# One more slot ahead of GpSimd's roots, and a residual load in sixteen pieces

## The chip, the cores and the metric

One core of a Trainium2 chip runs the kernel. The metric is device time in microseconds for one execution, from the start of the program to its end. A profile of one further execution shows what each engine did: PE (TensorE, matrix products; its weight loads are listed as PEld), DVE (VectorE), ACT (ScalarE), POOL (GpSimd), and SP (SyncE), which issues nearly all transfers.

## The reference

One layer of a hybrid streaming encoder is computed for 320 tokens: 256 of a new stream and 64 of a running one, model width 2048.

```python
h = rmsnorm(x, g_pre_mix)
p = h @ w_in                         # conv value and gate, q, k, v, z, two gates per head
a_out = conformer_conv(...)          # GLU, causal conv of width 31, LayerNorm per group, swish
b_out = gdn_mixer(...)               # gated delta rule, 8 heads of 128, chunks of 64
x = x + rmsnorm(concat(a_out, b_out) @ w_out, g_post_mix)
h = rmsnorm(x, g_pre_ffn)
gu = causal_dwconv(h @ w_up, ...)    # width 3
x = x + rmsnorm((silu(gate) * up) @ w_down, g_post_ffn)
```

Three pieces matter here. In the conv heads, eight groups of 128 channels are normalised per token: `(u - mu) * rsqrt(var + EPS)`. In the delta rule q and k are divided by their lengths, and its small matrices are scaled by `-beta` over the square of k's length. The output projection is followed by a norm, and then x, the residual stream, is added. All is fp32 in and out.

## The kernel before, in words

Each fp32 operand of a dense product is held as a rounded part (`whi`, `hh`, `bh`, ...) and a remainder (`wlo`, `hl`, `bl`, ...), and a product is three matmuls: hi by hi, hi by lo, lo by hi. Weights arrive by SP (L189) in blocks of 256 to 512 KB; ACT rounds a block to `whi` (L196), DVE subtracts to get `wlo` (L197). Three buffers hold raw blocks, three hold each split part, so the load of a block waits until `wlo` of the block three before it is done.

The order of the stages: the input projection, block by block (tiles psq, psv, psgate; up to about 433 us); the output projection `w_out` in two passes, the first with 11 of 16 k-blocks (psm, L212 to L216, up to about 512 us), the second with the last five (psm2, printed as psm, L999 to L1001); a norm; `w_up` with its conv; `w_down`; the last norm.

Everything that isn't a dense product runs as side jobs, written as generators. `tick` counts dense matmuls; after each 20 (GAP), it steps those jobs that are due. `yield wait, g, t` ends a step: the next one follows at the first count of 20 that is `wait` matmuls later, if g and t PSUM buffers of two pools can be held. What a step issues is then put in each engine's order by a scheduler that weighs its own estimates; what the engines run is one fixed list each, in order. So an instruction that waits holds all that stand behind it on its engine.

Four side jobs count here. `conv_tail` (one for each conv group, c0 to c7): three transposes into pt_c, statistics on DVE (L535, L536), EPS and the power -1/2 on GpSimd (L538, L539, tile grs), `gnm` on DVE (L541), three scalings on ACT (un, L544); after LAG_STAT = 100 matmuls, transposes back (pt_c2, L548), a swish on ACT (af, L550) and its split, bh on ACT (L220) and bl on DVE (L221), which the output projection reads. `gdn_tail` (eight heads, each in one or two parts; L645 runs eight times): transposes, square sums, EPS on DVE (L638, L639, tile tq), the power on GpSimd (L641, tile sc), small products on GpSimd (irk L643, cc L644, skd L646), snb on DVE (L645), scalings on ACT (kd L649, vh L654), matmuls pk and pks (L658, L662). The pair jobs solve the chunks (wi, np, tmp, dn: L666 to L706; zs L735, px L739, rhs L822, pvns L830, po L809 to L811, ks L839). `post` multiplies the heads' outputs by a root that GpSimd makes (L867 to L871), with the scalings at L873.

In the second pass of `w_out`, SP also carries x for the residual add (tile x1, L989), the first two blocks of `w_up` (printed with L189), and the parameters fpar of the next stage (L991). PSUM holds two psm2 blocks at a time: block n starts when DVE has added block n - 2 to its first half (m, L1007).

```python
hi, lo = load_split(ins["w_out2"][n], nk2 * P)
if n in (4, 8):
    upw.append(up_weights(len(upw), ugp))
```

Of the kernel before, what the change touches and what calls it, by code (L numbers as in the profile page):

```python
# [9 lines left out]
F32 = mybir.dt.float32  # L10
F32R = mybir.dt.float32r
AF = mybir.ActivationFunctionType
ALU = mybir.AluOpType
# [4 lines left out]
P = 128  # L18
D = 2048
KB = D // P  # L20
# [3 lines left out]
NH = 8  # L24
# [6 lines left out]
GAP = 20  # L31
# [8 lines left out]
LAG_NORM = 120  # L40
LAG_WAIT = 12
# [60 lines left out]
def trunk_kernel(ctx, tc, ins, outs):  # L102
    nc = tc.nc
# [188 lines left out]
    with tc.tile_pool(name="xp", bufs=1) as xp:  # L292
# [25 lines left out]
        with tc.high_priority(offset=PRI_E):  # L318
# [25 lines left out]
            for k in range(KB):  # L344
                x = xt[k // 4][:, k % 4, :]
# [52 lines left out]
    def gates():  # L398
# [54 lines left out]
        for t in (beta, eG, kdec):  # L453
            G.tensor_copy(t[0:TS, 2, 1:NH:2], t[0:TS, 2, 0:NH:2])
        G.tensor_scalar(neG, eG, -1.0, None, ALU.mult)
        for c, h0, w in ((0, 0, 4), (1, 0, 4), (2, 0, 8), (0, 4, 4), (1, 4, 4)):
            rg = gd.tile([P, 512], F32, tag="wtp", name="rg")
            eg = gd.tile([P, 512], F32, tag="wtp", name="eg")
            n = 512 // w
            if c < 2:  # L460
                rg3, mask = rg.rearrange("p (h i) -> p h i", i=n), cv("tri").unsqueeze(1).to_broadcast((P, w, n))
                g3 = gt[:, c, h0:h0 + w].unsqueeze(2).to_broadcast((P, w, n))
            else:
                rg3 = rg.rearrange("p (a b i) -> p a b i", b=2, i=n)
                mask = cv("tri2").rearrange("p (b i) -> p b i", b=2).unsqueeze(1).to_broadcast((P, 4, 2, n))
                g3 = gt[:, c, :].rearrange("p (a b) -> p a b", b=2).unsqueeze(3).to_broadcast((P, 4, 2, n))
            V.tensor_tensor(rg3, mask, g3, ALU.mult)
            yield LAG_DECAY, 1, 0
            psd = ps_g.tile([P, 512], F32, tag="g", name="psd")
            PE.matmul(psd, cv("strict"), rg, start=True, stop=True)  # L470
            S.activation(eg, psd, AF.Exp)
            for j in range(w // 2):
                if c < 2:
                    m = cv("tri").unsqueeze(1).to_broadcast((P, 2, n))
                else:
                    m = cv("tri2").rearrange("p (b i) -> p b i", b=2)
                V.tensor_tensor(E2[h0 // 2 + j][:, :, c * P:c * P + n],
                                eg[:, 2 * j * n:2 * (j + 1) * n].rearrange("p (b i) -> p b i", b=2), m, ALU.mult)
        gate.update(beta=beta, eG=eG, neG=neG, kdec=kdec, eGl=eGl, E=E)

    nqkv = const.tile([P, 24, 2, 3], F32, tag="nqkv", name="nqkv")

# [41 lines left out]
    def conv_tail(b, cvt, left):  # L524
# [13 lines left out]
        G.tensor_scalar(rs, gv[:, :, 1], EPS, None, ALU.add)  # L538
        G.tensor_tensor(rs, rs, nhalf[:, 0:3], ALU.pow)  # L539
        nm = cb.tile([P, 3], F32, tag="gnm", name="gnm")  # L540
        V.scalar_tensor_tensor(nm, gv[:, :, 0], -1.0, rs, ALU.mult, ALU.mult)  # L541
        un = cb.tile([P, 3, P], F32, tag="un", bufs=1, name="un")
        for c in range(3):
# [60 lines left out]
    def gdn_tail(h, st, kq, vT):  # L604
# [37 lines left out]
        rk, rq, irk, snb, cc, skd = (sc[:, i, :] for i in range(6))  # L642
        G.tensor_tensor(irk, tq6[:, 0, :], rk, ALU.mult)  # L643
        G.tensor_tensor(cc, rk, gate["beta"][:, 0:nch, h], ALU.mult)  # L644
        V.scalar_tensor_tensor(snb, cc, -1.0, rk, ALU.mult, ALU.mult)  # L645
        G.tensor_tensor(skd, rk, gate["kdec"][:, 0:nch, h], ALU.mult)  # L646
        for c in range(nch):
            if c < 2:
# [127 lines left out]
    def post(i, st):  # L776
# [92 lines left out]
        G.tensor_scalar(t1, t1, 1.0 / P, EPS, ALU.mult, ALU.add)  # L869
        G.tensor_tensor(t1, t1, nhalf[:, 0:NI], ALU.pow)  # L870
        G.tensor_tensor(t1, t1, rq, ALU.mult)  # L871
        for a in range(NI):
            S.activation(ot[:, a, :], ot[:, a, :], AF.Identity, scale=t1[:, a:a + 1])  # L873
        st["free"] = True
        yield LAG_NORM, 0, 2
        while any(zT[h] is None for h in hh_):
            yield GAP, 0, 2
        for s in range(2):
# [105 lines left out]
    for n in range(KB):  # L984
        hi, lo = load_split(ins["w_out2"][n], nk2 * P)
        if n in (4, 8):
            upw.append(up_weights(len(upw), ugp))
        if n < 8:
            nc.sync.dma_start(x1[:, 2 * n:2 * n + 2, :], ins["x"][:, 2 * n:2 * n + 2, :])  # L989
        elif n == 9:  # L990
            nc.sync.dma_start(fpar, ins["fpar"])  # L991
        whole = n == KB - 1
        psm = ps_p.tile([P, 512], F32, tag="p", name="psm2")
# [258 lines left out]
```

## Time and profile before

| | us |
|---|---|
| median of 3 runs (lowest, highest) | 1515.52 (1515.03, 1516.16) |
| the profiled execution | 1515.37 |
| its span in the trace | 1513.6 |
| PE busy | 1495.6 (99%) |
| DVE busy | 1007.1 (67%) |
| ACT busy | 736.2 (49%) |
| POOL busy | 280.0 (19%) |

The mean granted clock of TensorE is 0.998 of full speed. The span is what the trace covers of the profiled execution. A view of waits lists, for each engine, the idle time before an instruction and the instruction of another engine that ended it; the arrow points back to that one. A timeline lists start, length and, in brackets, the idle time before.

### The profile page before, as it was taken

What the parts mean: (1) busy time and instruction counts of PE and PEld (TensorE: products, weight loads), DVE (VectorE), ACT (ScalarE), POOL (GpSimd) and SP (SyncE); (2) the same over time, 40 slices, a digit from 0 to 9 for tenths busy, and PEclk for the clock granted to TensorE, in tenths of its full rate; (3) what the DMA queues carried; (4) which work ended last, traced back from release to release, by engine and by line L of the source; (5) the groups of instructions that cost most, each with busy time, mean ns of one, the idle gap of its engine ahead of it and who ended that gap; (6) DMA issues with size and microseconds to landing.
All of it is one profiled execution on the core that took longest, in us unless ns stands there. A gap on an engine that the chain in (4) does not pass through costs nothing.

```text
span 1513.6 us, 26743 instructions
## 1 busy us (share of the span) xinstructions
PE 1495.6 (99%) x10343; PEld 1470.5 (97%) x10344; DVE 1007.1 (67%) x1849; ACT 736.2 (49%) x1221; POOL 280.0 (19%) x460
## 2 busy tenths in 40 slices
PE   9999999999999999999999999999999999999998
PEld 8999999999999989999999999999999999999997
DVE  6779798889997568866435566445665545666554
ACT  7664656555554565544434444334444333444453
POOL 0323122330110000422002232001222101322101
PEclk9999999999999999999999999999999999999999
DMA  8435453445434663444455444455444455444453
GB/s 293 148 113 159 133 156 99 119 150 148 125 96 150 199 187 113 139 154 136 141 157 167 151 143 144 135 152 169 152 151 149 127 148 176 143 152 153 130 150 116
DMA packets 96983, 224.25 MB, mean 148 GB/s; under 512 B 18648, under 2 KB 37080, under 8 KB 96856
## 3 DMA queue, kind: packets, MB, share of 16 engines
q1 hardware_dynamic: 96712, 222.51, 47.5%
q8 instruction: 81, 1.33, 0.4%
q14 instruction: 46, 0.38, 0.1%
q10 hardware_dynamic: 144, 0.03, 0.0%
HBM read 215.39 MB, written 7.12 MB: 147 GB/s over the span
## 4 chain that ended last, share of the span: by engine, by line
PE 88%; DVE 6%; DMA 2%; ACT 1%; issue 1%; POOL 1%; ACTq 0%; DVEq 0%; SPq 0%; POOLq 0%
PE psu L212 13%; PE psu L213 13%; PE psu L216 13%; PE psdn L212 7%; PE psdn L213 7%; PE psdn L216 7%; PE psq L212 2%; PE psq L213 2%; PE psq L216 2%; DVE wlo L197 2%; DVE cvt L518 2%; PE ps_first L374 1%; PE psu L1054 1%; DMA w<-in_w_out 1%; PE psgate L216 1%; PE psv L216 1%
## 5 line engine op out<-in xcount | busy, mean ns | idle before, releaser
L196 ACT CAST whi<-w 128x1024 fp32r<-128x1024 f32 (+2 forms) x440 | 412.3, 940 | 512.0 <-PE psu L213 169.2
L197 DVE TENSOR_TENSOR wlo<-w,whi 128x1024 fp32r<-128x1024 f32 (+2 forms) x440 | 476.9, 1085 | 185.7 <-ACT whi L196 112.2
L212 PE MATMUL psu<-hi,whi 128*128 128x320 f32 x1344 | 397.1, 309 | 1.3 <-DVE fbuf L1089 1.3
L213 PE MATMUL psu<-lo,whi 128*128 128x320 f32 x1344 | 396.8, 309 | 0.0
L212 PEld LDWEIGHTS psu<-hi,whi 128*128 128x128 f32 x1344 | 252.2, 188 | 1.4 <-ACT rb L1071 1.4
L213 PEld LDWEIGHTS psu<-lo,whi 128*128 128x128 f32 x1344 | 252.3, 188 | 0.0
L216 PE MATMUL psu<-hi,wlo 128*128 128x320 f32 x1344 | 224.4, 309 | 0.0
L1090 POOL COPY nffn<-fbuf 128x2 f32<-128x2 f32 x88 | 102.4, 1164 | 589.0 <-DVE fbuf L1088 584.6
L213 PE MATMUL psdn<-gl,whi 128*128 128x320 f32 x704 | 208.9, 309 | 0.0
L216 PEld LDWEIGHTS psu<-hi,wlo 128*128 128x128 f32 x1344 | 204.0, 188 | 0.0
L212 PE MATMUL psdn<-gh,whi 128*128 128x320 f32 x512 | 152.4, 309 | 0.0
L1088 DVE TENSOR_TENSOR fbuf<-psu,rb 128x256 f32<-128x256 f32 x88 | 37.3, 424 | 170.3 <-PE psu L216 170.3
L518 DVE SCALAR_TENSOR_TENSOR cvt<-ub,par,cvt 128x350 f32<-128x350 f32 x240 | 136.5, 586 | 2.9 <-ACT cvt L517 0.3
L213 PEld LDWEIGHTS psdn<-gl,whi 128*128 128x128 f32 x704 | 132.1, 188 | 0.3
L212 PE MATMUL psq<-hh,whi 128*128 128x320 f32 x352 | 107.0, 317 | 0.0
L213 PE MATMUL psq<-hl,whi 128*128 128x320 f32 x352 | 104.1, 309 | 0.0
L212 PEld LDWEIGHTS psdn<-gh,whi 128*128 128x128 f32 x512 | 96.1, 188 | 0.0
L216 PE MATMUL psdn<-gh,wlo 128*128 128x320 f32 x512 | 95.9, 309 | 0.0
L216 PEld LDWEIGHTS psdn<-gh,wlo 128*128 128x128 f32 x512 | 80.3, 188 | 0.0
L212 PEld LDWEIGHTS psq<-hh,whi 128*128 128x128 f32 x352 | 66.1, 188 | 0.7 <-issue 0.5
L213 PEld LDWEIGHTS psq<-hl,whi 128*128 128x128 f32 x352 | 66.1, 188 | 0.6 <-issue 0.5
L1132 DVE TENSOR_TENSOR y<-y,psdn 128x320 f32<-128x320 f32 x48 | 23.4, 488 | 63.6 <-PE psdn L216 63.6
(341 smaller groups left out, 2468.8 us busy)
## 6 DMA issues: line engine op xcount, KB each, us to landing
w<-in_w_up SPq DMA_DIRECT2D x176, 512.0 KB, 3.8
w<-in_w_in SPq DMA_DIRECT2D x88, 512.0 KB, 3.7
w<-in_w_down SPq DMA_DIRECT2D x64, 384.0 KB, 3.1
w<-in_w_down SPq DMA_DIRECT2D x64, 320.0 KB, 3.0
w<-in_w_out SPq DMA_DIRECT2D x32, 320.0 KB, 2.9
w<-in_w_out SPq DMA_DIRECT2D x16, 384.0 KB
w<-in_w_first SPq DMA_DIRECT2D x6, 512.0 KB, 5.8
wtp<-wsp SPq DMA_DIRECT2D x4, 640.0 KB
```

The costliest lines, as they stand in the source:

```text
L196: S.copy(hi[:, 0:width], w[:, 0:width])
L197: V.tensor_tensor(lo[:, 0:width], w[:, 0:width], hi[:, 0:width].bitcast(F32), ALU.subtract)
L212: tick(PE.matmul(ps, wh, xh, start=(k0 + j == 0), stop=False))
L213: tick(PE.matmul(ps, wh, xl, start=False, stop=False))
L216: tick(PE.matmul(ps, lo[:, j * P:(j + 1) * P], xh, start=False, stop=(final and k0 + j == nk - 1)))
L374: tick(PE.matmul(ps, w, xh, start=(k == 0 and wt is hi), stop=(k == KB - 1 and wt is lo)))
L518: return lambda: V.scalar_tensor_tensor(cvt, ub[:, t:t + 350], pv("w_dw", b * 31 + t), cvt, ALU.mult, ALU.add)
L1054: PE.matmul(pss[i][:, 0:T], w, xh, start=(k == 0 and part == "h"), stop=(k == KB - 1 and part == "l"))
L1088: V.tensor_tensor(buf[:, 2:258], psu[:, 0:TP], rb2[:, 0:TP], ALU.mult)
L1090: G.tensor_copy(nffn[:, b, 0, :], buf[:, 256:258])
L1132: V.tensor_tensor(y[:, n, :], y[:, n, :], psd[:, 0:T], ALU.add)
```

## The change

Four edits. In `gdn_tail`, snb is made by two operations on GpSimd from a new constant nbeta (minus beta, made once), and the DVE operation L645 goes. In `conv_tail`, a yield stands between GpSimd's power and `gnm`, so `gnm` and un belong to the next step, and the transposes back follow 100 matmuls after that. In `post`, a yield stands ahead of the scalings L873, and the wait behind them is 20 shorter. In the second pass of `w_out`, x comes in sixteen pieces of 160 KB, one for each block, instead of eight of 320 KB in the first eight blocks; fpar is written behind the last.

```diff
--- before.py
+++ after.py
@@ -453,6 +453,8 @@
         for t in (beta, eG, kdec):
             G.tensor_copy(t[0:TS, 2, 1:NH:2], t[0:TS, 2, 0:NH:2])
         G.tensor_scalar(neG, eG, -1.0, None, ALU.mult)
+        nbeta = const.tile([P, 3, NH], F32, tag="nbeta", name="nbeta")
+        G.tensor_scalar(nbeta, beta, -1.0, None, ALU.mult)
         for c, h0, w in ((0, 0, 4), (1, 0, 4), (2, 0, 8), (0, 4, 4), (1, 4, 4)):
             rg = gd.tile([P, 512], F32, tag="wtp", name="rg")
             eg = gd.tile([P, 512], F32, tag="wtp", name="eg")
@@ -476,7 +478,7 @@
                     m = cv("tri2").rearrange("p (b i) -> p b i", b=2)
                 V.tensor_tensor(E2[h0 // 2 + j][:, :, c * P:c * P + n],
                                 eg[:, 2 * j * n:2 * (j + 1) * n].rearrange("p (b i) -> p b i", b=2), m, ALU.mult)
-        gate.update(beta=beta, eG=eG, neG=neG, kdec=kdec, eGl=eGl, E=E)
+        gate.update(beta=beta, nbeta=nbeta, eG=eG, neG=neG, kdec=kdec, eGl=eGl, E=E)
 
     nqkv = const.tile([P, 24, 2, 3], F32, tag="nqkv", name="nqkv")
 
@@ -538,6 +540,7 @@
         G.tensor_scalar(rs, gv[:, :, 1], EPS, None, ALU.add)
         G.tensor_tensor(rs, rs, nhalf[:, 0:3], ALU.pow)
         nm = cb.tile([P, 3], F32, tag="gnm", name="gnm")
+        yield LAG_WAIT, 0, 1
         V.scalar_tensor_tensor(nm, gv[:, :, 0], -1.0, rs, ALU.mult, ALU.mult)
         un = cb.tile([P, 3, P], F32, tag="un", bufs=1, name="un")
         for c in range(3):
@@ -642,7 +645,8 @@
         rk, rq, irk, snb, cc, skd = (sc[:, i, :] for i in range(6))
         G.tensor_tensor(irk, tq6[:, 0, :], rk, ALU.mult)
         G.tensor_tensor(cc, rk, gate["beta"][:, 0:nch, h], ALU.mult)
-        V.scalar_tensor_tensor(snb, cc, -1.0, rk, ALU.mult, ALU.mult)
+        G.tensor_tensor(snb, rk, gate["nbeta"][:, 0:nch, h], ALU.mult)
+        G.tensor_tensor(snb, snb, rk, ALU.mult)
         G.tensor_tensor(skd, rk, gate["kdec"][:, 0:nch, h], ALU.mult)
         for c in range(nch):
             if c < 2:
@@ -869,10 +873,11 @@
         G.tensor_scalar(t1, t1, 1.0 / P, EPS, ALU.mult, ALU.add)
         G.tensor_tensor(t1, t1, nhalf[:, 0:NI], ALU.pow)
         G.tensor_tensor(t1, t1, rq, ALU.mult)
+        st["free"] = True
+        yield LAG_WAIT, 0, 0
         for a in range(NI):
             S.activation(ot[:, a, :], ot[:, a, :], AF.Identity, scale=t1[:, a:a + 1])
-        st["free"] = True
-        yield LAG_NORM, 0, 2
+        yield LAG_NORM - GAP, 0, 2
         while any(zT[h] is None for h in hh_):
             yield GAP, 0, 2
         for s in range(2):
@@ -985,9 +990,8 @@
         hi, lo = load_split(ins["w_out2"][n], nk2 * P)
         if n in (4, 8):
             upw.append(up_weights(len(upw), ugp))
-        if n < 8:
-            nc.sync.dma_start(x1[:, 2 * n:2 * n + 2, :], ins["x"][:, 2 * n:2 * n + 2, :])
-        elif n == 9:
+        nc.sync.dma_start(x1[:, n:n + 1, :], ins["x"][:, n:n + 1, :])
+        if n == KB - 1:
             nc.sync.dma_start(fpar, ins["fpar"])
         whole = n == KB - 1
         psm = ps_p.tile([P, 512], F32, tag="p", name="psm2")
```

Behind a change of this kind the scheduler lays out every engine anew. Below, before and after, are three places; an L number is that of its own kernel, so L544 before and L547 after are the same line, as are L809 and L813, L548 and L551, L839 and L843, L947 and L952, L989 and L993.

ACT at the end of conv group c6's statistics, in the first pass of the output projection (whi: rounded weights; m: a finished block copied out); before:

```order
L947 COPY m_5644<-psm 128x320
L196 CAST whi<-w 128x640
L544 ACTIVATE un<-pt_c,gnm,grs 128x128 x3
L947 COPY m_5721<-psm 128x320
L196 CAST whi<-w 128x768
L196 CAST whi<-w 128x640
L196 CAST whi<-w 128x768
L947 COPY m_5773<-psm 128x320
```

After:

```order
L952 COPY m_5654<-psm 128x320
L196 CAST whi<-w 128x640
L196 CAST whi<-w 128x768
L952 COPY m_5731<-psm 128x320
L547 ACTIVATE un<-pt_c,gnm,grs 128x128 x3
L196 CAST whi<-w 128x640
L196 CAST whi<-w 128x768
L952 COPY m_5783<-psm 128x320
```

The three un stood ahead of one copy of m and of the rounding of a 768-wide block; now both stand ahead of un.

PE where the transposes back of conv group c4 stand (pt_c2 reads un; bh4 is what comes of it), at the end of the input projection; before:

```order
L809 MATMUL po_5113<-vn_5070,kd_3687 128x128
L548 MATMUL pt_c2_5127<-cst_82,un_4930 128x128
L809 MATMUL po_5113<-vn_5070,kd_3687 128x128
L548 MATMUL pt_c2_5127<-cst_82,un_4930 128x128
L811 MATMUL po_5113<-vn_5070,at_3689 128x128
L548 MATMUL pt_c2_5127<-cst_82,un_4930 128x128
L811 MATMUL po_5113<-vn_5070,at_3689 128x128
L830 MATMUL pvns_5121<-rhs_5078,wtp_4169 128x128
L212 MATMUL psv_5046<-hh12_102,whi_5101 128x320
L213 MATMUL psv_5046<-hl12_118,whi_5101 128x320
```

After:

```order
L216 MATMUL psv_5056<-hh14_104,wlo_5112 128x320
L216 MATMUL psv_5056<-hh15_105,wlo_5112 128x320
L551 MATMUL pt_c2_5156<-cst_82,un_4963 128x128 x3
L212 MATMUL psm_5173<-bh0_2340,whi_5176 128x320
L213 MATMUL psm_5173<-bl0_2341,whi_5176 128x320
L212 MATMUL psm_5173<-bh1_3254,whi_5176 128x320
L213 MATMUL psm_5173<-bl1_3255,whi_5176 128x320
L843 MATMUL ks1_5184<-sn0_5128,kq_3411 128x128
```

The transposes stood among the po matmuls, ahead of the last sixteen psv matmuls; now they stand behind these, right before the first block of the output projection.

SP's issues in the second pass (x is tile x1, w a weight block); before:

```order
L189 DMA w<-in_w_out 128x640 x6
L989 DMA x_6120<-in_x 128x640
L189 DMA w<-in_w_up 128x4x256
L989 DMA x_6120<-in_x 128x640 x2
L189 DMA w<-in_w_out 128x640
L989 DMA x_6120<-in_x 128x640
L189 DMA w<-in_w_out 128x640 x2
L989 DMA x_6120<-in_x 128x640
L189 DMA w<-in_w_out 128x640
L989 DMA x_6120<-in_x 128x640
L189 DMA w<-in_w_up 128x4x256
```

After:

```order
L189 DMA w<-in_w_out 128x640 x6
L189 DMA w<-in_w_up 128x4x256
L993 DMA x_6130<-in_x 128x320 x5
L189 DMA w<-in_w_out 128x640
L993 DMA x_6130<-in_x 128x320 x2
L189 DMA w<-in_w_out 128x640 x2
L993 DMA x_6130<-in_x 128x320
L189 DMA w<-in_w_out 128x640
L993 DMA x_6130<-in_x 128x320 x2
L189 DMA w<-in_w_up 128x4x256
L189 DMA w<-in_w_out 128x640
```

The first block of `w_up` now stands ahead of the first x; five pieces of 160 KB stand ahead of the next block of `w_out` where two loads of 320 KB stood, behind a third ahead of `w_up`.

In that stretch ACT and DVE also split the first `w_up` block ahead of block n = 4 of `w_out`, where they split n = 4 first. Elsewhere: `gnm` stands in the same place of DVE's order as before at the px matmuls of 326 us; both rhs operations (L822) of the pair at 362 us stand ahead of the reduction L698 that runs at 359.77 us; pt_o and pz matmuls stand 24 matmuls further ahead of the px matmuls of 397 us; c7's transposes back stand right behind the last block of the first pass, where eleven of its matmuls followed them.

## Rows read from the trace of the kernel before

**Rows 1.** The page's first part: busy us, share of the span, instructions.

```profile
PE 1495.6 (99%) x10343; PEld 1470.5 (97%) x10344; DVE 1007.1 (67%) x1849; ACT 736.2 (49%) x1221; POOL 280.0 (19%) x460
```

**Rows 2.** PE's waits: instruction <- what ended it: us in total, times, longest.

```profile
PE px L739 <- DVE zs L735: 3.5, 2, 3.0
PE psm L999 <- DVE m L1007: 1.6, 3, 1.1
...
PE psm L212 <- ACT whi L196: 1.3, 1, 1.3
PE pks L662 <- ACT vh L654: 1.0, 1, 1.0
PE pvns L830 <- DVE rhs L822: 0.7, 1, 0.7
```

**Rows 3.** DVE's waits, first 605 us.

```profile
DVE sc L645 <- POOL sc L644: 10.8, 7, 1.9
DVE gnm L541 <- POOL grs L539: 9.9, 8, 2.6
```

**Rows 4.** Timeline, head 1: start, us, engine, line, operation, [idle before].

```profile
108.93 1.19 POOL L582 COPY nqkv<-qb 128x3 f32<-128x3 f32 x1
...
110.45 0.16 DVE L639 TENSOR_SCALAR tq<-ssq 128x3 f32<-128x3 f32 x1
...
110.69 1.33 POOL L641 TENSOR_TENSOR sc<-tq,nhalf 128x6 f32<-128x6 f32 x1 [0.58 <-DVE tq L639]
...
112.32 0.37 ACT L654 ACTIVATE vh<-tv,sc 128x128 f32<-128x128 f32 x1 [2.52 <-POOL sc L643]
```

**Rows 5.** GpSimd's groups by form: busy us, mean ns, idle before.

```profile
L582 POOL COPY nqkv<-qb 128x3 f32<-128x3 f32 x24 | 12.2, 510 | 0.0
...
L646 POOL TENSOR_TENSOR sc<-sc,kdec 128x2 f32<-128x2 f32 x4 | 0.8, 196 | 0.0
```

**Rows 6.** Timeline of DVE before the px wait of 3.02 us.

```profile
323.98 0.16 DVE L541 SCALAR_TENSOR_TENSOR gnm<-gvar,grs 128x3 f32<-128x3 f32 x1 [1.10 <-POOL grs L539]
...
325.65 0.48 DVE L735 TENSOR_TENSOR zs<-pz,cst 128x320 f32<-128x320 f32 x1
```

**Rows 7.** Timeline of DVE before the pvns wait.

```profile
359.77 0.34 DVE L698 TENSOR_REDUCE wi<-tmp 40x14 f32<-40x98 f32 x1
...
361.98 0.36 DVE L822 SCALAR_TENSOR_TENSOR rhs<-ks,neG,vh 64x128 f32<-64x128 f32 x1
```

**Rows 8.** Timeline of DVE before the second px wait.

```profile
396.98 0.48 DVE L735 TENSOR_TENSOR zs<-pz,cst 128x320 f32<-128x320 f32 x1
```

**Rows 9.** Timeline of ACT at the first psm wait.

```profile
480.23 1.16 ACT L544 ACTIVATE un<-pt_c,gnm,grs 128x128 f32<-128x128 f32 x3 [5.31 <-DVE gnm L541]
...
481.58 2.22 ACT L196 CAST whi<-w 128x768 fp32r<-128x768 f32 x3
```

**Rows 10.** Timeline, all engines, first blocks of the output projection.

```profile
428.75 1.28 ACT L550 ACT_TABLE_LOAD   x1
...
434.55 0.21 DVE L509 TENSOR_TENSOR ub<-psv,sg 128x64 f32<-128x64 f32 x1
...
435.69 0.31 PE L212 MATMUL psm<-bh,whi 128*128 128x320 f32 x1
```

**Rows 11.** Timeline of ACT, second pass of the output projection.

```profile
518.45 1.05 ACT L196 CAST whi<-w 128x1024 fp32r<-128x1024 f32 x1 [0.66 <-DMA w<-in_w_up]
...
521.85 0.73 ACT L196 CAST whi<-w 128x640 fp32r<-128x640 f32 x1 [1.38 <-DMA w<-in_w_out]
...
530.55 1.67 ACT L196 CAST whi<-w 128x1024 fp32r<-128x1024 f32 x2 [0.89 <-DMA w<-in_w_up]
```

**Rows 12.** SP's queue in the same stretch.

```profile
513.81 0.38 SPq L189 DMA_DIRECT2D w<-in_w_up  x1
...
516.47 0.33 SPq L189 DMA_DIRECT2D w<-in_w_out  x1
...
525.06 0.38 SPq L189 DMA_DIRECT2D w<-in_w_up  x1
```

## What the change does to the time, predicted

> **What bounds the kernel now.** I read the page's first part, then PE's waits, then, for each wait, the timeline of the engine that ends it. PE is busy 1495.6 us of a 1513.6 us span [rows 1], so an edit counts only where it moves a moment at which PE stands still. The waits of PE that the change can reach add up to 3.5 + 1.6 + 1.3 + 1.0 + 0.7 = 8.1 us [rows 2]: px for DVE's zs, psm for DVE's m and for ACT's whi, pks for ACT's vh, pvns for DVE's rhs. The rest of PE's idle time lies at the start, in the norm between the projections, and at the end, where nothing is edited. DVE stands 10.8 us before L645 and 9.9 us before gnm, both for GpSimd [rows 3], but DVE is idle a third of the span; those 20.7 us are no estimate of the gain. The ceiling is 8.1 us, or 0.5%.
>
> **The change part by part.** All sums are against the profiled execution's 1515.37 us, which is 0.15 us under the median of 1515.52.
>
> The operation at L645 leaves DVE eight times. Only one of its waits reaches PE. In head 1 the chain is DVE's L639 at 110.45, GpSimd's power at 110.69 (it stood 0.58 us for L639), then vh on ACT at 112.32, which stood 2.52 us [rows 4], and pks on PE, 1.0 late [rows 2]. Without the wait of the first part, 10.8 / 7 = 1.5 us on average [rows 3], L639 comes some 1.4 us sooner, but the power can't start before GpSimd's copy at 108.93 is over, at 110.12, which is 0.57 before 110.69 [rows 4]; that copy starts sooner too, since DVE feeds it. So the gain lies between 0.57 and 1.0 before what comes in its place; 0 is the weak end, since the copy's start is not certain.
>
> In its place GpSimd gets two operations of 0.20 us each, going by their like, L646 [rows 5]. One stands ahead of skd, one behind it. Behind skd waits kd on ACT, and ACT's order here is vh, kd, kd, vh, where pks reads the last vh; so what skd loses, pks loses: 0.15, the pitch of these operations. A third, 128x24, is made once at the gates, at 0. The first term is 0.8 - 0.15: I take -0.65 (-0.85 to +0.2). The row beside it shows what could go wrong: three-element copies on GpSimd take 0.51 us on average [rows 5], and the one at 108.93 took 1.19 [rows 4], against 0.20 for the products.
>
> The Trainium skill (GPSIMD Engine Reference, Specifications) says that GpSimd's way into SBUF is shared with VectorE and contended when VectorE reads two SBUF inputs, as many of DVE's operations here do. If by that rule the new operation ahead of skd took 1.19 and not 0.20, the term would be +0.35, and the whole time 1.0 longer; the four rows of L646, with a mean of 0.196 beside the same DVE work, don't bear it out.
>
> The wait inside the conv tail does not do at the largest stop what its words suggest. px at 326 us waits 3.0 us [rows 2] for zs, which starts at 325.65, behind gnm, which stood 1.10 for GpSimd's power [rows 6]. In the changed order gnm has the same place on DVE, so that 1.10 stays. What is left is that L645 of the head before no longer stalls DVE some 12 us earlier, most of which is taken up by a later wait for ACT. Bounds: -1.10 if gnm's wait were to go by luck, +0.15 if nothing does; I take -0.4.
>
> Two other stops go by the new order. rhs at 361.98 makes pvns 0.7 late; it now stands ahead of the reduction of 359.77 [rows 7], two microseconds sooner, so the whole 0.7 goes (0 if the pair's tiles come later). zs at 396.98 [rows 8] makes px 3.5 - 3.0 = 0.5 late [rows 2]; with the pt_o matmuls ahead, PE has work in that gap: -0.45 (0 at worst).
>
> The psm wait of 1.3 [rows 2] is the clearest. ACT stood 5.31 us at un, for gnm, and the 768-wide rounding that PE needed ran only at 481.58 [rows 9]. It now stands ahead of un, in time in which ACT idled. -1.3; what is late next is un, and its transposes come 100 matmuls later.
>
> New stops. c4's transposes now stand right before the first block of the output projection. PE asks for bh at 435.69 now [rows 10]; in the new order one pair of matmuls is put ahead, so at about 436.0, and for bl about 0.7 later, at 436.7. To get there ACT must load a table (1.28) [rows 10] behind a rounding that ends near 433.4: 433.4 + 1.3 = 434.7, then af 0.5, cvt 0.5, bh 0.5, so bh is done at 436.2; DVE's bl, behind ub (ends at 434.76) [rows 10], a 768-wide wlo, rh, ot and s, ends at about 437.2. So +0.5 (0 to 1.1). At c7 the transposes stand right before the second pass, and bh and bl must be there within 9 and 12 matmuls, 1.3 and 1.8 us; af, bh and bl need about 2.0: +0.3 (0 to 0.7).
>
> The second pass is bound by loads. w_up's first block, issued at 513.81, is rounded at 518.45, 4.6 later; the w_out block issued at 516.47 at 521.85, 5.4 later; w_up's second, 525.06, at 530.55, 5.5 later [rows 11, 12]. ACT waited for all three to land, and the last, through DVE's in-order queue, makes the 1.1 us of the psm waits for m; those waits sum to 1.6 [rows 2]. Halving x takes 160 KB off each block and, with the third load gone from there, some 320 KB from ahead of w_up's second block, about 1 us at some 270 KB a microsecond (an estimate: between 516.47 and 521.85 what was left of 512 + 640 KB and the 320 KB of the block itself, 1472 KB in 5.4 us at most). Against it, w_up's first block is now split ahead of n = 4 of w_out; so n = 4's wlo ends near 521.2 instead of 518.7, and the load of n = 6, which waits for that buffer, leaves 2.5 us later. PE wants n = 6 at 526.4; issued at 521.2 into an emptier queue (4 us) it is split by about 526, just in time, but w_up's second block then goes 0.8 later, and the 1 us is spent. I take 0 (-1.6 to +4.9, the latter from the rival below).
>
> The Trainium skill (DMA: Bandwidth & Descriptors, Bandwidth) has the rule to batch transfers, with 32% of peak at 64 KB and 78% at 1 MB, and (same page, Anatomy of one DMA) a fixed 2.0 us for each; paid one after another, eight more issues would be an estimated 16 us, and the time 1528.6. The trace doesn't bear that out: two loads issued 2.66 us apart landed 3.40 apart, each taking over 4.6 us [rows 11, 12], so they overlap.
>
> The later yield in the post job keeps the sum of its waits at 120 and moves ACT's scalings only; where they stood ACT had cover. 0.
>
> Sum: -0.65 - 0.4 - 0.7 - 0.45 - 1.3 + 0.5 + 0.3 + 0 = -2.7. From 1515.37 that is 1512.7; by the median 1512.8, which I predict.
>
> **The rivals.** *The loads relieve PE too.* If n = 6 comes in time and w_up's second block 1 us sooner, most of the 1.6 us of m waits goes as well: -2.7 - 1.4 = -4.1, 1511.4. For it: less x in the queue just there. Against it: the later load of n = 6.
>
> *The order gives back what it took.* px at 326 gains nothing, head 1 only 0.5, new stops at c4 and c7 at 1.0 and 0.6: -0.5 - 0.7 - 0.45 - 1.3 + 1.6 = -1.35, or less if a stop of that kind comes where I saw none; 1514.3. For it: gnm's place is unchanged, and the new layout was made on estimates, as the old was, which left 8.1 us.
>
> *Slower: the second pass starves.* If w_up's first block takes 5.5 us, as its second did, it is rounded at 519.3; n = 4 is rounded behind it at 521.4 and its wlo ends at 523.0, 4.4 late. n = 6 then needs 5.4 more, and DVE adds block m only behind its wlo, at 530.8 instead of 526.4. w_up's second load waits for that buffer and comes 4.9 late. The price is +4.9, and the sum -2.7 + 4.9 = +2.2: 1517.7. It decides from 2.7 us on. For it: both long latencies are in these rows. Against it: w_up now goes with no x ahead of it.
>
> **How the numbers follow.** The forecast has 0.45, within 1511.8 to 1514.0; the relief 0.20; the give-back 0.25; the starved pass 0.10. A measurement of this kernel can tell 0.2%, 3.0 us, from no change: faster means under 1512.5. Of the forecast's 0.45 a little under half lies there, 0.19, and nearly all of the relief: 0.39 faster. The starved pass lies above 1518.5 with about half its chance, and unseen stops add a little: 0.07 slower. Within: 0.54. The range runs from the relief's lower side to short of the starved pass: 1510.4 to 1516.6.
>
> **What would show it.** Right: no wait of psm for whi near 481, none of pvns near 362, px near 326 still over 2.3 us; pks near 113 under 0.4; small new waits at bh or bl near 436 and 513. Wrong: px near 326 down by over 1 us, or waits of psm for whi, wlo or m between 520 and 537 that differ from 1.6 by more than 1 us.

## The result, and the profile after

The change makes the kernel slower. Its median is 1520.36 us (1518.0 to 1523.97, 7 runs) beside 1515.57 for the kernel before on the same chip: a ratio of 1.0035, 95% interval 1.0026 to 1.0045. I had predicted 1512.8, a range of 1510.4 to 1516.6, and 0.07 for slower. The profiled execution of after took 1520.29 us, its span is 1518.5 (before: 1513.6), and the mean granted clock 0.995 (0.998).

The page's first part answers to [rows 1]: engine, busy us, share, instructions.

```profile
PE 1498.7 (99%) x10343; PEld 1474.5 (97%) x10344; DVE 1008.2 (66%) x1841; ACT 736.7 (49%) x1221; POOL 284.7 (19%) x477
```

PE runs the same 10343 matmuls and is busy 3.1 us longer, so part of the loss is not standing still but running slower. PE's waits, to be held beside [rows 2] (instruction <- what ended the wait: us in total, times, longest):

```profile
PE px L743 <- DVE zs L739: 4.9, 2, 3.1
PE pks L666 <- ACT vh L658: 2.0, 1, 2.0
PE pvns L834 <- DVE rhs L826: 1.4, 1, 1.4
...
PE psm L1003 <- DVE m L1011: 1.2, 1, 1.2
...
PE psm L213 <- DVE bl L221: 0.4, 1, 0.4
```

The wait of psm for whi is gone, as is the old stop of pvns at 362. But pks waits 2.0 instead of 1.0, the second px 1.8 instead of 0.5, and pvns has a new stop at 196. The granted clock stands in the eighth place of the view by windows (stretch, length, busy time of five engines, PEclk, DMA share, GB/s):

```profile
100.00:150.00 50.00, 48.05 (x315) 47.26 (x314) 44.61 (x100) 26.99 (x73) 16.93 (x37) 0.97 0.44 133
300.00:350.00 50.00, 46.92 (x350) 45.71 (x350) 41.10 (x84) 23.67 (x61) 18.80 (x27) 0.93 0.41 125
400.00:450.00 50.00, 47.80 (x374) 45.68 (x373) 47.69 (x92) 26.96 (x51) 3.24 (x4) 0.97 0.34 98
```

Before, these three read 1.00, 0.97 and 1.00. Each of the three holds a stop of PE of 1.8 us or more, and the matmuls behind it run at the lower of the two clock levels (half clock, below). PE's timeline at the first of them:

```profile
113.87 0.93 PE L666 MATMUL pks<-kqs 128*128 128x256 f32 x2 [1.95 <-ACT vh L658]
114.24 0.83 PE L212 MATMUL psq<-hh,whi 128*128 128x320 f32 x1
114.87 0.47 PE L213 MATMUL psq<-hl,whi 128*128 128x320 f32 x1
115.13 0.47 PE L212 MATMUL psq<-hh,whi 128*128 128x320 f32 x1
...
118.31 0.31 PE L212 MATMUL psz<-hh,whi 128*128 128x320 f32 x1
```

The same place before:

```profile
113.57 0.70 PE L662 MATMUL pks<-kqs 128*128 128x256 f32 x2 [1.00 <-ACT vh L654]
...
116.45 0.31 PE L212 MATMUL psz<-hh,whi 128*128 128x320 f32 x1
```

A 320-column matmul that elsewhere ends 0.31 us after its start takes 0.47 here, and the next one starts 0.267 later instead of 0.147. From pks to the first matmul of the next block (psz) it is 118.31 - 113.87 = 4.44 us; before, 116.45 - 113.57 = 2.88. The stop costs 0.95 more, and the half clock behind it 1.56 more.

Stop by stop, after less before (us): head 1 +0.95 and +1.56; pvns at 196 +1.4; px at 326, where the stop is unchanged (3.02 to 3.06), +1.6 of half clock behind it; the second px +1.3 and some 1.1 of half clock (eight L216 matmuls took 2.48, elsewhere 1.33); bl +0.4. Against that: an earlier start, there within the first 20 us, -0.64; another order of PE's small matmuls near 186, -0.85; pvns at 362, -0.8; psm at 481, -1.4; the second pass, -0.95. That is 8.3 - 4.6 = 3.7 of the span's 4.9; the rest is spread over small differences.

Not all of this is shown to be the change's. Before's own profile has a short half-clock stretch at px: its window from 300 to 350 us reads 0.97, but that of e4_x16, e2_conv and stand_kept below, whose times are before's, reads 0.93 as after's does. So the 1.6 at px may be a difference between runs. Before's runs beside all these experiments, some 130, have a mean of 1514.4 at a granted clock of 0.999 and of 1516.7 at 0.996. What after loses isn't all of that kind: its one run at 0.998 took 1518.0, and before's 34 runs at 0.998 have a mean of 1515.2.

### The profile page after: what moved, and what is told of

The parts are those of the page before. It is cut to its first block, busy times and chain, and to the rows that moved or that the text cites. A ratio compares the mean times of both kernels' runs of the same rounds, so it can differ in the third digit from the quotient of the medians.

```text
span 1518.5 us, 26776 instructions
## 1 busy us (share of the span) xinstructions
PE 1498.7 (99%) x10343; PEld 1474.5 (97%) x10344; DVE 1008.2 (66%) x1841; ACT 736.7 (49%) x1221; POOL 284.7 (19%) x477
## 3 DMA queue, kind: packets, MB, share of 16 engines
q8 instruction: 81, 1.33, 0.4%
## 4 chain that ended last, share of the span: by engine, by line
PE 86%; DVE 8%; DMA 2%; ACT 1%; issue 1%; POOL 1%; SPq 0%; DVEq 0%; ACTq 0%; POOLq 0%
PE psu L212 13%; PE psu L213 13%; PE psu L216 13%; PE psdn L212 7%; PE psdn L213 7%; PE psdn L216 7%; DVE cvt L520 2%; DVE wlo L197 2%; PE psq L216 2%; PE psq L212 2%; PE psq L213 2%; PE psm L216 2%; PE psm L213 2%; PE psm L212 2%; PE psu L1058 1%
## 5 line engine op out<-in xcount | busy, mean ns | idle before, releaser
L216 PE MATMUL psu<-hi,wlo 128*128 128x320 f32 x1344 | 224.4, 309 | 0.0
L216 PEld LDWEIGHTS psu<-hi,wlo 128*128 128x128 f32 x1344 | 204.1, 188 | 0.0
L216 PE MATMUL psdn<-gh,wlo 128*128 128x320 f32 x512 | 95.9, 309 | 0.0
L216 PEld LDWEIGHTS psdn<-gh,wlo 128*128 128x128 f32 x512 | 80.3, 188 | 0.0
```

The lines of the kernel that those rows point to most:

```text
L216: tick(PE.matmul(ps, lo[:, j * P:(j + 1) * P], xh, start=False, stop=(final and k0 + j == nk - 1)))
```

## The experiments

All were timed beside the kernel before on the same chip; "ratio" is to its runs there, with a 95% interval.

**Which part loses.** e1_snb is the snb hunks of the diff alone, e2_conv the yield in `conv_tail` alone, e4_x16 the sixteen loads alone. The yield in `post` has no run of its own; after_stand_skd below holds it beside the other parts.

```diff
e1_snb:  -  V.scalar_tensor_tensor(snb, cc, -1.0, rk, ALU.mult, ALU.mult)
         +  G.tensor_tensor(snb, rk, gate["nbeta"][:, 0:nch, h], ALU.mult)
         +  G.tensor_tensor(snb, snb, rk, ALU.mult)
e2_conv: +  yield LAG_WAIT, 0, 1
e4_x16:  -  if n < 8: ... x1[:, 2 * n:2 * n + 2, :]
         +  nc.sync.dma_start(x1[:, n:n + 1, :], ins["x"][:, n:n + 1, :])
```

Expected of e1_snb: 

> Only snb moves to GpSimd; the rest is the kernel before. Theory (the new operation ahead of skd lengthens GpSimd's chain, and what goes by the clock is larger than the stop itself): the wait of pks near 113 grows from 1.0 to about 2.0, the granted clock falls behind it for some 3 us, and the time is 1.5 to 3 us above before, 1517.0 to 1518.5. Rival (the loss is all in the conv tail's new order; GpSimd's part is what I predicted): pks under 0.5, 1514.5 to 1515.5.

Expected of e2_conv: 

> Only the yield ahead of gnm in the conv tail. Theory (the new order puts DVE's conv work ahead of what the pairs wait for): pvns near 196 stands over 1 us, px near 397 about 1.8 us instead of 0.5 with a low clock behind it, the wait of psm for whi near 481 and of pvns near 362 gone; together +1 to +4 us, 1516.5 to 1519.5. Rival (those stops come only with the later start that head 1 gives): px near 397 about 0.5, no stop near 196, and 1.5 to 2.5 us under before, 1513 to 1514.

Expected of e4_x16: 

> Only the sixteen pieces of x. Theory (less x beside the weights in the second pass): waits of psm for m fall from 1.6 to about 1.2 in total and little else changes, -0.3 to -1.2 us, 1514.3 to 1515.2. Rival (the first block of w_up ahead of n = 4 starves n = 6): +1 to +5 us.

Measured: e1_snb 1519.19, ratio 1.0032 (1.002 to 1.0044); e2_conv 1514.73, 0.9999 (0.999 to 1.0007); e4_x16 1515.53, 1.0006 (0.9997 to 1.0015). The snb part alone has the whole loss, more than the 1517.0 to 1518.5 expected, with pks at 1.93 and half clock behind it. e2_conv lies in neither range: the stops are nearly those of the theory, the time is before's. The yield does remove the stops at 481 and 362, as I said, and gets others in their place, at 196, 398 and 439. e4_x16 changes nothing that can be told; its waits for m are 1.9, where I expected 1.2. e2_conv's waits:

```profile
PE px L740 <- DVE zs L736: 3.5, 2, 2.3
...
PE pvns L831 <- DVE rhs L823: 1.3, 1, 1.3
```

**How moving one small product can cost 5 us: the place of skd.** In head 1 of after, GpSimd and the engines that wait for it (start, us, engine, line, operation, [idle before]):

```profile
104.03 1.36 POOL L644 TENSOR_TENSOR sc<-tq,nhalf 128x4 f32<-128x4 f32 x1 [3.49 <-DVE tq L642]
...
105.46 0.31 POOL L646 TENSOR_TENSOR sc<-tq,sc 128x2 f32<-128x2 f32 x1
105.74 0.19 POOL L647 TENSOR_TENSOR sc<-sc,beta 128x2 f32<-128x2 f32 x1
105.89 0.51 POOL L648 TENSOR_TENSOR sc<-sc,nbeta 128x2 f32<-128x2 f32 x1
106.36 0.19 POOL L650 TENSOR_TENSOR sc<-sc,kdec 128x2 f32<-128x2 f32 x1
...
110.48 1.33 POOL L644 TENSOR_TENSOR sc<-tq,nhalf 128x6 f32<-128x6 f32 x1 [3.42 <-DVE tq L642]
...
112.34 0.56 POOL L650 TENSOR_TENSOR sc<-sc,kdec 128x3 f32<-128x3 f32 x1
```

```profile
106.59 0.37 ACT L653 ACTIVATE kd<-tkq,sc 128x128 f32<-128x128 f32 x1 [2.17 <-POOL sc L650]
...
112.93 0.62 ACT L653 ACTIVATE kd<-tkq,sc 128x128 f32<-128x128 f32 x2 [0.45 <-POOL sc L650]
```

```profile
108.53 0.17 DVE L641 TENSOR_SCALAR tq<-ssq 128x3 f32<-128x3 f32 x1 [1.72 <-ACT vh L637]
```

And before:

```profile
104.67 1.36 POOL L641 TENSOR_TENSOR sc<-tq,nhalf 128x4 f32<-128x4 f32 x1 [3.48 <-DVE tq L639]
...
106.65 0.37 ACT L649 ACTIVATE kd<-tkq,sc 128x128 f32<-128x128 f32 x1 [1.58 <-POOL sc L646]
...
112.40 0.20 POOL L646 TENSOR_TENSOR sc<-sc,kdec 128x3 f32<-128x3 f32 x1
```

DVE no longer stands for GpSimd. ACT does, at kd, 2.17 us instead of 1.58; the square sums of the next part are behind kd in ACT's order, and DVE stands 1.72 for them. So the second power starts 6.45 behind the first (110.48 - 104.03), where before it was 6.02 (110.69 - 104.67): +0.43. From there to the end of skd it is 2.42 (112.90 - 110.48) instead of 1.91 (112.60 - 110.69): +0.51. Both together, 0.94, are the stop's 0.95.

Three kernels move skd: e5_skd_first is after with skd ahead of both snb products (the orders of PE, ACT and DVE are after's), snb_skd_first the same in the snb part alone, and snb_extra puts two more products in the snb part, which leaves snb without its second factor.

```diff
e5_skd_first, snb_skd_first:
+        G.tensor_tensor(skd, rk, gate["kdec"][:, 0:nch, h], ALU.mult)
         G.tensor_tensor(snb, rk, gate["nbeta"][:, 0:nch, h], ALU.mult)
         G.tensor_tensor(snb, snb, rk, ALU.mult)
-        G.tensor_tensor(skd, rk, gate["kdec"][:, 0:nch, h], ALU.mult)
snb_extra:
+        G.tensor_tensor(snb, rk, gate["nbeta"][:, 0:nch, h], ALU.mult)
+        G.tensor_tensor(snb, rk, gate["nbeta"][:, 0:nch, h], ALU.mult)
```

Expected of e5_skd_first: 

> The changed kernel with skd made ahead of snb's two operations on GpSimd; every other engine's order is the same. Theory (skd's delay makes head 1's stop, and the stop the low clock): pks near 113 back to 1.0 to 1.3, clock full behind it, and 2 to 2.7 us under the changed kernel, 1517.5 to 1518.5. Rival (GpSimd's operations are slow there whatever their order, because DVE is busier): pks stays near 2.0, 1520.

Expected of snb_skd_first: 

> Only snb moves to GpSimd, as in the run of that part alone, but skd is made ahead of it; the order of PE, DVE and ACT is that of that run. Theory (the operation ahead of skd costs some 3 of the 4.2 us, the lost stand of DVE the rest): pks 1.2 to 1.4, full clock behind it, 1516.3 to 1517.5. Rival (the place of skd matters only beside the conv tail's new order): 1519.

Expected of snb_extra: 

> As the run of snb alone, with one more operation of the same kind ahead of skd (snb's first product made twice); nothing else moves. Theory (what delays skd delays kd, and all behind kd on ACT): GpSimd's chain is 0.15 to 0.5 us longer in each part, pks 2.1 to 2.8, ACT's waits for skd grow by 1 to 3 us over the eight parts, 1519.7 to 1522. Rival (skd has room): 1519.2, pks 1.9.

Measured: e5_skd_first 1516.84, 1.001 (1.0001 to 1.0019), pks 1.26 and full clock behind it, a gain larger than expected; snb_skd_first 1518.15, 1.0017 (1.0008 to 1.0025), pks 1.29, above the 1516.3 to 1517.5 expected. Moving skd back ahead of the two products takes 0.25% off after, and 0.15% off the snb part. snb_extra missed its aim: its two products stand behind skd in GpSimd's order, and it came out as e1_snb, 1519.84, 1.0027 (1.0016 to 1.0039), pks 1.96. Two more products behind skd cost nothing that shows here.

**What is left: the lost stand of DVE.** no_snb has a constant in place of snb (it leaves out that product): the DVE operation goes and nothing comes to GpSimd. stand_kept has snb on GpSimd behind skd, and a small DVE copy that reads cc in L645's old place, of use to nobody; after_stand is after with that copy, after_stand_skd after with the copy and skd first.

```diff
no_snb:     -  V.scalar_tensor_tensor(snb, cc, -1.0, rk, ALU.mult, ALU.mult)
            +  snb = small_c[:, 0:nch]
stand_kept, after_stand, after_stand_skd:
               G.tensor_tensor(cc, rk, gate["beta"][:, 0:nch, h], ALU.mult)
            +  skw = gd.tile([P, 3], F32, tag="skw", name="skw")
            +  V.tensor_copy(skw[:, 0:nch], cc)
```

Expected of no_snb: 

> The kernel before without snb: a constant stands in its place, so DVE loses L645 and GpSimd gets nothing for it. Theory (two causes: an operation ahead of skd, and GpSimd slower while DVE works on instead of standing at L645): only the second is left, so the power and the products in head 1 are up to 0.6 us longer than in the kernel before, pks stands 0.9 to 1.4, and the time is 0 to 1.5 us above before. Rival (only the operation ahead of skd does it): pks at 0.5 or less and 1 to 2 us under before.

Expected of stand_kept: 

> The snb product on GpSimd behind skd, as in snb_skd_first, but in L645's place in VectorE's order stands a small copy that reads cc, so VectorE waits there as before. Theory (VectorE's stand at L645 keeps GpSimd's small products at 0.20 us and the order of the engines behind it as before): stop at pks about 1.0 us, stop at px of pair 2 about 3.0, time 1515 to 1516, ratio 0.999 to 1.001. Rival (the loss is snb's own place on GpSimd, or of VectorE's code that moved): ratio 1.0015 to 1.0020 as snb_skd_first and no_snb.

Expected of after_stand: 

> The kernel after with a small VectorE copy that reads cc at the place that L645 had before, and nothing else changed: TensorE's, ScalarE's and GpSimd's orders are those of after. Theory (VectorE's stand behind cc keeps GpSimd's products short, 0.20 us, so skd comes some 0.3 us sooner, and the order of VectorE behind it is before's): stop at pks 1.1 to 1.3 us and no half-clock stretch behind it, time 1516 to 1517, ratio 1.0005 to 1.0012. Rival (the two products ahead of skd cost the same with or without the stand): pks about 1.9 with half clock behind it, ratio 1.002 to 1.0025.

Expected of after_stand_skd: 

> The kernel after with the same copy and skd ahead of the two snb products on GpSimd: both causes undone, all else of the change kept. Theory: pks about 1.0 us, ratio as that of the yields and the loads alone, 0.9995 to 1.0007. Rival (the three parts of the change add a loss together that none has alone): ratio 1.001 or more, as e5_skd_first.

Measured: no_snb 1517.52, 1.0015 (1.0006 to 1.0023), 2.0 above before where 0 to 1.5 was expected: taking the operation out altogether, with its wait, is a loss. stand_kept 1515.19, 1.000 (0.9991 to 1.0008): with an operation that does nothing but wait, snb_skd_first's loss is gone. One rival is left in this: with the copy a few DVE instructions between 128 and 139 us, and one of DVE and one of ACT at 325 us, also stand in another place than in snb_skd_first, and no run separates that order from the wait. In head 1 the two orders are the same but for the copy. after_stand 1516.64, 1.0007 (0.9998 to 1.0016); after_stand_skd 1515.44, 1.0002 (0.9993 to 1.0011). On the kernel after, then: neither repair 1.0035, skd first 1.0010, the stand 1.0007, both 1.0002. The two don't add up; either one alone takes pks back to 1.1 to 1.3, and most of the loss goes. The rivals named ahead of these runs fell: snb on GpSimd costs nothing by itself, and the parts have no loss together that none has alone. GpSimd in head 1 of stand_kept, to be held beside the rows of after:

```profile
105.37 0.20 POOL L645 TENSOR_TENSOR sc<-tq,sc 128x2 f32<-128x2 f32 x1
105.53 0.20 POOL L646 TENSOR_TENSOR sc<-sc,beta 128x2 f32<-128x2 f32 x1
105.68 0.20 POOL L649 TENSOR_TENSOR sc<-sc,kdec 128x2 f32<-128x2 f32 x1
...
109.95 1.33 POOL L643 TENSOR_TENSOR sc<-tq,nhalf 128x6 f32<-128x6 f32 x1 [0.58 <-DVE tq L641]
...
111.66 0.20 POOL L649 TENSOR_TENSOR sc<-sc,kdec 128x3 f32<-128x3 f32 x1
```

While DVE stands each product takes 0.20; in head 1 of after, where DVE works on, some take 0.31 to 0.56. They are not slowed evenly. In after's whole trace eleven products take over 0.30, and each of them ends 0.04 to 0.06 us after a cvt, a wlo or a tmp of DVE that runs beside it. The longest:

```profile
275.01 1.17 POOL L649 TENSOR_TENSOR sc<-sc 128x3 f32<-128x3 f32 x1
```

```profile
274.88 1.26 DVE L197 TENSOR_TENSOR wlo<-w,whi 128x1024 fp32r<-128x1024 f32 x1
```

In these rows such a product costs what is left of DVE's instruction when it starts; two that began while DVE read a PSUM tile (106.36 beside qb, 112.04 beside at) took 0.19 to 0.20. In stand_kept the second power starts 6.01 behind the first one again, and skd ends 1.91 behind its start: the two figures of before. The skd product by form, over the four parts that have it (busy us, mean ns | idle before), first after, then stand_kept:

```profile
L650 POOL TENSOR_TENSOR sc<-sc,kdec 128x3 f32<-128x3 f32 x4 | 1.4, 362 | 0.0
```

```profile
L649 POOL TENSOR_TENSOR sc<-sc,kdec 128x3 f32<-128x3 f32 x4 | 0.8, 195 | 0.0
```

What stays open is where all of no_snb's and snb_skd_first's 0.15% lies. Their profiled runs took 1515.69 and 1516.46, 1.7 to 1.8 us under their medians, and show only longer stops at pks (1.0 to 1.3) and at the first px (3.0 to 3.7 and 3.8), 1.0 to 1.1 us. snb_skd_first's:

```profile
PE px L742 <- DVE zs L738: 4.2, 2, 3.7
```

snb_skd_again was to be snb_skd_first once more, but the kernel that ran under its label was snb_extra's, so it settles nothing about that: 1520.68 in one run, with snb_extra's stops (pks 1.9, px 4.0). Its expectation was: 

> snb_skd_first once more, for another profile: its profiled run took 1516.46, its median 1518.15. Theory (what its median has over that run is half clock behind a stop that is only sometimes there): in a run of 1518 or more the stops are those of the first profile within 0.3 us, and a stretch of half clock behind pks or px is 1.5 us or more longer. Rival (another order of arrivals): a stop is 1 us or more longer. In a run of under 1517 nothing is told apart.

**The half clock.** w_before puts 18 products of 320 columns, which nothing reads, ahead of the first px in the kernel before; w_after puts 8, 18 and 10 of this kind into the three stops of after (pks and the two px).

```diff
+        for _ in range(st["warm"]):
+            PE.matmul(px, wz[:, 0:P], wz[:, 0:NI * 64]..., start=True, stop=True)
+            if h == 1:
+                keep_warm(pks, 8)
```

Expected of w_before: 

> The kernel before with 18 matmuls on zeros of 320 columns in the stop before px of pair 2 (3.0 us), PE's order otherwise the same. Theory (as above): the slow matmuls behind px near 329 to 331 run at full clock and 1 to 1.8 us go: 1513.2 to 1514.0. Rival: no change, 1515.0.

Expected of w_after: 

> The changed kernel with matmuls on zeros (nothing reads them) in PE's three long stops: 8 of 512 columns before pks of head 1, 18 and 10 of 320 columns before px of pairs 2 and 3. They are shorter than the stops. Theory (the lowered clock behind a long stop is a cost of its own): the granted clock stays full behind all three, the stops themselves keep their ends, and the time falls by 3 to 5 us, to 1515.3 to 1517.3. Rival (the loss is the waiting alone): no change, 1520.

Measured: w_before 1514.65, 0.9998 (0.9989 to 1.0006), the rival's time. The clock did rise: eleven of its twelve runs have a mean of 0.999 or 1.000, where before's lie at 0.996 to 0.999. What that gave was lost again. Where it was lost can be read from one profile alone, that of its slowest run (1519.14): the half clock behind px is gone and the px stops are 0.9 in all, but pvns at 362 waits 3.2 instead of 0.7 and is followed by half clock.

```profile
PE pvns L834 <- DVE rhs L826: 3.2, 1, 3.2
...
PE px L743 <- DVE zs L737: 0.9, 2, 0.6
```

w_after 1523.82, 1.0056 (1.0043 to 1.0069), is slower than after and missed both expectations. It is no test of the clock at pks: the products there waited for vh themselves (2.0) and came after the stop. At the two px the stops fell from 3.1 and 1.8 to 0.7 and 0.4, but in its profile (1525.62) a pks at 345 waits 2.4 and a px of zq at 418 1.4, which after doesn't have, with half clock behind each.

**Is DVE's pace what makes the stops come back?** px_late is the `conv_tail` yield with px of two pairs one slot later. taps25_before and taps25_after are the two kernels with 25 of 31 taps of each conv chain on DVE (they leave out six taps).

```diff
px_late:  -  yield LAG_WAIT, 2, 0
          +  yield LAG_WAIT + st["late"], 2, 0
taps25:   -  taps.extend((left, tap(t)) for t in range(31))
          +  taps.extend((left, tap(t)) for t in range(25))
```

Expected of px_late: 

> The yield in the conv tail alone, and px of pairs 2 and 3 one slot of 20 matmuls later. If stops of PE and the clock behind them are the whole story, both px waits (2.3 and 1.2 us with that yield) and the low clock behind the first (about 2 us) go, -4 to -6 us against that yield alone: 1509 to 1511. Rival (the pair's chain is itself late, so the wait moves to the next product, py, zq or the po matmuls): within 1 us of 1514.7.

Expected of taps25_before: 

> The kernel before with 25 of the 31 taps of each convolution chain on VectorE (leaves out six taps of each). About 48 VectorE operations of about 0.59 us less each, nothing else changed. Theory (VectorE sets the pace between 300 and 450 us, where it is 85 to 94% busy): the stops at px of pair 2 (3.0 us), pvns and the second px go, and the half-clock stretch behind the first; time 1509 to 1512, ratio 0.996 to 0.998. Rival (the stops are an order's, one chain that is late in one place): px of pair 2 keeps over 2 us, ratio 0.999 to 1.001.

Expected of taps25_after: 

> The kernel after with the same six taps of each chain left out. Theory: as in taps25_before the stops at 300 to 450 us go; what is left over taps25_before is head 1, the stop at pks of about 1.9 us and the half clock behind it, so 1512 to 1515, about 2 to 3 us over taps25_before. Rival (the change's loss is the px stops' alone): equal to taps25_before within 1 us.

Measured: px_late 1516.81, 1.001 (1.0001 to 1.0018), outside both ranges: in its profile, that of its slowest run (1519.53), the stop moved on to the px of zq, 4.1. taps25_before 1514.47, 0.9991 (0.9982 to 1.0); taps25_after 1517.62, 1.0009 (1.0001 to 1.0018). taps25_before's wait of px, its first 605 us, and its DVE ahead of the first px:

```profile
PE px L739 <- DVE zs L735: 4.0, 2, 2.9
```

```profile
0.00:605.00 605.00, 594.19 (x4231) 575.68 (x4232) 468.72 (x954) 348.08 (x699) 102.30 (x195) 0.99 0.49 149
```

```profile
319.69 2.43 DVE L518 SCALAR_TENSOR_TENSOR cvt<-ub,par,cvt 128x350 f32<-128x350 f32 x4
...
326.02 0.49 DVE L735 TENSOR_TENSOR zs<-pz,cst 128x320 f32<-128x320 f32 x1
```

DVE is busy 468.7 us there instead of 491.1, 22 us less, and px still waits 2.9. So a lighter DVE alone doesn't take the stops away, and that much of my theory fell. What sets them is not settled. With fewer taps the order is another: no gnm stands near the first px (it runs at 283.2), and DVE works without a stand from 312.29 to zs, though pz, which zs reads, is done at 320.7. There it is DVE's own work, in its order, that makes px wait. In after, as in before, zs stands behind gnm, which waits for GpSimd's power, but of the 3.06 that is 1.09; the last rows are those of the second px:

```profile
326.68 0.16 DVE L544 SCALAR_TENSOR_TENSOR gnm<-gvar,grs 128x3 f32<-128x3 f32 x1 [1.09 <-POOL grs L541]
...
328.36 0.48 DVE L739 TENSOR_TENSOR zs<-pz,cst 128x320 f32<-128x320 f32 x1
...
401.64 0.54 DVE L890 SCALAR_TENSOR_TENSOR zo<-pt_o,par,zT 128x320 f32<-128x320 f32 x1
402.10 0.48 DVE L739 TENSOR_TENSOR zs<-pz,cst 128x320 f32<-128x320 f32 x1
```

taps25_after is 3.15 us over taps25_before (expected: 2 to 3, at 1512 to 1515, which it missed), so the change costs some 3 us with a lighter DVE too. In its profile pks waits 1.95, as in after, and no half clock follows:

```profile
114.51 0.70 PE L666 MATMUL pks<-kqs 128*128 128x256 f32 x2 [1.95 <-ACT vh L658]
114.86 0.50 PE L212 MATMUL psq<-hh,whi 128*128 128x320 f32 x1
115.19 0.31 PE L213 MATMUL psq<-hl,whi 128*128 128x320 f32 x1
```

That execution took 1515.85 against a median of 1517.62. So behind a stop of this length the fall may or may not come: at the pks of head 1 it came in four of the five profiles with a stop of 1.9 to 2.0 and full work behind it, and in none with 1.3 or less.

**A better kernel?** skd_vh_first is before with skd ahead of cc on GpSimd and the vh scalings ahead of kd on ACT; yield_skd_vh adds the `conv_tail` yield.

```diff
+        G.tensor_tensor(skd, rk, gate["kdec"][:, 0:nch, h], ALU.mult)
         G.tensor_tensor(cc, rk, gate["beta"][:, 0:nch, h], ALU.mult)
...
+        for c in range(nch):
+            S.activation(vh[:, i0 + c, :], tvs[c], AF.Identity, scale=irk[:, c:c + 1])
```

Expected of skd_vh_first: 

> The kernel before, with skd made ahead of cc on GpSimd and, on ACT, all vh of a part ahead of its kd; DVE's and PE's orders are the same. Theory (pks waits behind kd, and kd behind skd): pks falls from 1.0 to 0.3 to 0.7, and 0.3 to 1.5 us go: 1513.5 to 1515.0. Rival (DVE's L645, which waits for cc, now 0.15 us later each time, gives it back): 1515 to 1516.

Expected of yield_skd_vh: 

> The same two edits on the kernel with the conv tail's yield alone. Theory: they add up, 1513.0 to 1514.5, under both kernels. Rival (what PE gains before 200 us it waits for again behind DVE between 300 and 450 us): within 0.5 us of 1514.7.

Measured: 1515.1, 0.9996 (0.9987 to 1.0005), and 1515.19, 0.9998 (0.9988 to 1.0007). pks waits 0.59 in both, 0.4 less than before, as it should, but the times are those of the rivals: neither can be told from before's. No version that does the whole work beat the kernel before by more than a measurement shows.

## Why the prediction was wrong

The step that failed is the first term of the sum, head 1, for which I took -0.65 (-0.85 to +0.2). It measured +0.95 at the stop and +1.56 behind it: +2.5, and with it the sign of the whole. e1_snb, which has only this part of the change, has the whole loss. Of my signs of being right most came (no wait near 481 or 362, px near 326 over 2.3, a small one at bl); pks under 0.4 did not, and no sign of being wrong looked at head 1.

- *"L639 comes some 1.4 us sooner."* Counted from the first power of the head, it came 0.4 later. I removed DVE's wait and looked at what DVE would do next, not at who else waited for the same engine: kd on ACT was the next in line for GpSimd, ACT's square sums stood behind kd, and DVE needs those. The wait didn't go, it went to ACT and came back.
- *"What skd loses, pks loses: 0.15."* The mechanism was right (products behind skd are free, one ahead is paid by pks), the size wrong: 0.51. I took L646's 0.20 [rows 5] as the price "beside the same DVE work", but before, L643 to L646 ran mostly while DVE stood at L645. The copy of 1.19 [rows 4], which ends 0.06 behind DVE's wlo, showed the other price. The same copy took 0.19 in after, while DVE stood for ACT:

```profile
106.75 0.18 POOL L584 COPY nqkv<-qb 128x3 f32<-128x3 f32 x1
106.88 0.19 POOL L585 COPY nqkv<-qb 128x3 f32<-128x3 f32 x1
```

The rule of the Trainium skill that I set aside (GPSIMD Engine Reference, Specifications: a path into SBUF shared with VectorE) agrees with these rows; the row with which I refuted it had been measured in the shelter that the change took away.

- *The granted clock had no term.* A stop was priced at its length. In after's profile the kernel pays again behind three stops: 1.56 at pks, some 1.1 at the second px, and 1.6 more than before at the first, which may be a difference between runs.
- *px at 326, -0.4.* The stop didn't change, but not because nothing touched it: with the yield alone it is 2.3, with the snb part alone 4.4. That L645 no longer stalls DVE, from which I took the -0.4, did not shorten it. Why the snb part lengthens it stays open.
- *pvns at 362, -0.7, and psm at 481, -1.3.* Both went, with some 0.8 and 1.4. ACT's rounding now runs ahead of un:

```profile
484.43 0.83 ACT L196 CAST whi<-w 128x768 fp32r<-128x768 f32 x1 [2.37 <-DMA w<-in_w_out]
...
487.95 0.46 ACT L547 ACTIVATE un<-pt_c,gnm,grs 128x128 f32<-128x128 f32 x1 [2.37 <-DVE gnm L544]
```

- *The second px, -0.45.* +1.3 and half clock: the pt_o matmuls that I put into its gap ran before it, and on DVE a zo that reads them stands ahead of zs. pvns at 196, +1.4, I did not see at all.
- *bl, +0.5:* 0.4, at 443. *c7, +0.3:* no stop there.
- *The loads, 0.* Right for the time: 1.0006. The starved second pass did not come; the waits for m are 1.2 instead of 1.6.

Of the rivals, the one that gives back what it took was nearest in kind (e2_conv shows just that for the yield: two stops gone, others come, 0.9999), but it left head 1 a gain. Contention on GpSimd, which I set aside, had the loss in the right place; priced for one product at +0.35, it would have given 1513.7, still a gain. Two sums are off by 0.1, and nothing hangs on them: the give-back's 1514.3 is 1514.2 (1515.52 - 1.35), the 1528.6 is 1528.7.

## What to carry to other kernels

A wait on an engine that isn't the bottleneck may be what shelters another's work: before removing it, ask who else waits for the same producer, and whether the producer runs faster because the waiting engine is still. Order a slow helper's products by who stands behind each, the one that feeds the critical chain first. Where a stop of the bound engine is removed, price the next one of the same chain, and look in the trace for what a stop costs behind itself, in clock, before pricing it at its length.

## What the runs showed of the hardware

- In head 1 GpSimd's products on 128x2 or 128x3 took 0.19 to 0.20 us while VectorE stood and up to 0.56 while it worked, a copy of 128x3 0.19 and 1.19. The longest product of after took 1.17. All eleven over 0.30 end 0.04 to 0.06 behind an instruction of VectorE that runs beside them.
- TensorE fell to the lower level (a 320-column matmul each 0.267 instead of 0.147) behind stops of 1.35 (w_after) to 4.4 us (e1_snb), but not behind each: 1.95 at pks in taps25_after and 1.68 at px in e5_skd_first were not followed by it. After dense work had resumed, it lasted 2.3 us in before (first px), some 3.5 in after (pks) and 5.2 in after_stand (second px).
- Runs of one kernel differ by it: after_stand's ranged from 1513.5 (granted clock 0.998) to 1518.71 (0.995), and the profiled 1518.71 has 18 matmuls in a row at half clock behind its second px stop.
- A copy of 0.17 us that only waits, with the order that the scheduler gives beside it, was worth 2.6 us (snb_skd_first 1.0017, stand_kept 1.000).
